# Routing map of a decoder step on one core: a job's tiles evicted one job later, a unit's weights split between its quarters

## The chip, the core and the metric

The kernel runs on one core of a Trainium2 chip. A core has a matrix engine (PE, with its weight loads listed apart as PEld), a vector engine (DVE), a scalar engine (ACT), a general engine (POOL) and a queue engine (SP). Each takes its instructions in order, and they meet at semaphores. The metric is the device time of one execution in microseconds (us).

## The reference

One decoder layer for 256 prompt tokens and 64 sample tokens. Attention and a gating unit come first; then a layer of 16,384 small experts, of which every token uses 16 for each of 8 heads; then a gated embedding. The part that matters here is the expert layer:

```python
s1, s2 = q1 @ k1.T, q2 @ k2.T                    # 128 keys each
v1, i1 = top_k(s1, 16);  v2, i2 = top_k(s2, 16)
sc, ci = top_k(all pairs v1 + v2, 16)
e = i1[ci // 16] * 128 + i2[ci % 16]             # expert of a pair of keys
g = softmax(sc)
out = sum over e of  g * gelu(u_tab[e] . x) * v_tab[e]
```

## The kernel before

For 240 prompt tokens the kernel does not gather experts. It goes through all of them densely: 128 "u" units give the activations of 128 experts each for all tokens, 128 "v" units multiply them back, and a routing map of tokens by experts, zero almost everywhere, weighs them in between. The map must stand in device memory before the first activations are weighed.

A unit is one 1 MB tile of weights (`w_raw`). `prepare(n, h)` fetches it at h = 0 by SP's queue and makes, for half h, a high part (`w_hi`, ACT, L683) and the rest (`w_lo`, DVE, L684), so that a product of three matmuls (`mm3`, L98 to L100) has full precision. A pool of four holds the halves' parts. `multiply(n, h, q)` does quarter q of half h: four chunks of three matmuls. A half is called a slot here, slot = 2n + h; the stage has 28 units, so slots 0 to 55. `finish(n)` takes a unit's sum through the activation function on ACT (L706).

The map is made in slots 42 to 55, in 30 jobs of 8 tokens. Job j has three steps:

- `one_hots(j)`: DVE compares the chosen keys with all keys (`e`, L762) and weighs the result (`p`, L763). Two buffers of each.
- `map_products(j)`: 16 short matmuls on PE (L775) into two tiles of PSUM, of the tag "s" for even and "o" for odd jobs; each tag has two buffers.
- the eviction, in the same function: two ACT instructions (L779) move the two tiles into half of `g_st`, a tile for 16 tokens with two buffers. After an odd job POOL writes `g_st` to device memory, `gd` (L786). The eviction into a buffer of `g_st` waits for the write of two tiles before.

The order is written out by hand: instructions of PE, DVE and ACT stand on each engine as the code issues them (`manual_schedule`, L931). In a slot with map jobs the loop goes over the two quarters: `multiply`, then (in a unit's first quarter) `finish` of the unit before, then for each job that is due `one_hots(job + 1)` and `map_products(job)` with its eviction. Behind both quarters stands `prepare` of the slot three ahead (L953). Jobs are due evenly: one in a quarter, and in two of the 28 quarters two.

Behind the stage four more units run without jobs; then the first tile of the map is read back (`fetch_g`, L839) and its activations weighed (`weights`, L842), and the long part with u and v units begins.

Of the kernel before, what the change touches and what calls it, by code (L numbers as in the profile page):

```python
# [52 lines left out]
def _build(ctx, tc, nc, a):  # L53
# [16 lines left out]
    def psum(tag, cols, parts=P):  # L70
        t = ps.tile([P, 512], F32, tag=tag, name="ps_" + tag)
        return t[:parts, :cols]
# [598 lines left out]
    def prepare(n, h):  # L671

        if h == 0:
            r = raw.tile([P, 16, P], F32, name="w_raw")
            o = order[n]
            src = a["uT"][o[1]] if o[0] == "u" else a["v_t"][o[1], o[2]]
            nc.sync.dma_start(r.rearrange("p a b -> p (a b)"), src)
            halves[n] = [r]
        r = halves[n][0]
        hi = hl.tile([P, 8, P], F32R, name="w_hi")  # L680
        lo = hl.tile([P, 8, P], F32R, name="w_lo")
        s = r[:, 8 * h : 8 * h + 8]
        act.activation(hi, s, AF.Copy)  # L683
        vec.tensor_sub(lo, s, hi.bitcast(F32))  # L684
        halves[n].append((hi, lo))
# [79 lines left out]

    def map_products(j):
        e, parts = oh.pop(j)
        tb, hb = divmod(j, 16 // NB)
        if hb == 0:
            oh["st"] = oh["pool"].tile([P, NK, 16], F32, name="g_st")  # L770
        for q in range(NB // 4):
            gp = psum("so"[j % 2], 512)
            for t in range(4):
                for k in range(2):
                    pe.matmul(  # L775
                        gp[:, t * P : t * P + P], e[:, 1, q, :, t], parts[:, k, q, :, t], start=k == 0, stop=k == 1
                    )
            b = hb * NB + 4 * q
            act.activation(  # L779
                oh["st"][:, :, b : b + 4].rearrange("p a t -> p t a"),  # L780
                gp.rearrange("p (t a) -> p t a", t=4),
                AF.Copy,
                scale=1.0 / WSC,
            )
        if hb == 16 // NB - 1:
            pool.dma_start(  # L786
                gd[:, :, tb * P : tb * P + P].rearrange("g p x -> p g x"),
                oh["st"].rearrange("p (g i) t -> p g (i t)", g=NG),
            )
# [125 lines left out]
    def front():  # L915

        for c in heads[6:]:
            yield from c
        yield from soften()
        picks = key_tables()  # L920
        yield 1.4
        shut(c_rt)
        state["xc"], state["xcp"] = open_pool("xc")
        xcp = state["xcp"]
        state["rows"] = [xcp.tile([P, D], F32, name=n) for n in ("xc", "xx")]
        state["xd"] = lambda: xcp.tile([P, P], F32, name="xd", bufs=2)
        open_tables(picks)
        yield 1.4
        one_hots(0)

    with tc.manual_schedule(engines={mybir.EngineType.DVE, mybir.EngineType.Activation, mybir.EngineType.PE}):  # L931
        for n in range(2):
            for h in range(2):
                prepare(n, h)


        steps, spent, job, first = front(), 0.0, 0, None
        for n in range(U1):
            for h in range(2):
                slot = 2 * n + h  # L940
                for q in range(2):
                    multiply(n, h, q)
                    if h == 0 and q == 0 and n:
                        finish(n - 1)
                    if first:
                        at_ = (2 * (slot - first) + q + 1) / (2 * (2 * U1 - first))
                        while job < JOBS and job < round(JOBS * at_):
                            if job + 1 < JOBS:
                                one_hots(job + 1)
                            map_products(job)  # L950
                            job += 1
                if first:
                    prepare((slot + 3) // 2, 1 - h)  # L953
                else:
                    while steps and spent < 1.4 * (slot + 1):
                        cost = next(steps, None)
                        if cost is None:
                            steps = None
                        else:
                            spent += cost  # L960
                    if steps:
                        prepare(n + 2, h)
                    else:
                        first = slot + 1
        prepare(U1 + 1, 1)
        n = U1
        shut(oh["close"])
        c_vp, vp = open_pool("vp")
        c_xc, (xc, xx) = state["xc"], state["rows"]
        tails = []  # L970
        for z in (A0, C):
            z = z[2][:, :, :, TP : TP + TD // 4].rearrange("p c h t -> p (c h) t")
            tails += [[z[:, 4 * k : 4 * k + 4] for k in (2 * i, 2 * i + 1)] for i in range(2)]
        sets = [
            Rows("c", c_e, c_g, xc, rcol[:, 2:3]),
            Rows("x", x_eg[:, 0].bitcast(I32), x_eg[:, 1], xx, rcol[:, 3:4]),
        ]
        steps = [(k, j, second) for second in (False, True) for k in sets for j in range(k.n)]
        rows = {}

        def row(m):
            if m < len(steps):
                k, j, second = steps[m]
                rows[m] = k.fetch(j, second)


        state["g"] = fetch_g(0, pool)
        to_c = rows_of(xc, state["xd"], slice(TP, T), 2)
        to_x = rows_of(xx, state["xd"], slice(0, XT), PH)
        load = weights(0, state["g"])  # L990
        for n in range(n, LEAD):
            finish(n - 1)
            for h in range(2):
                for q in range(2):
                    multiply(n, h, q)
                    next(to_c, None)
                if 2 * (n - U1) + h >= 4:
                    for _ in range(3):
                        next(load, None)
                if n == LEAD - 1 and h == 0:  # L1000
                    for m in range(3):
                        row(m)
                prepare(n + 2, h)
        for _ in to_c:
            pass


        END = len(order) - 10
        extra = lambda n: 0.65 * (order[n - 1][0] == "v")
        step_us = 2.4  # L1010
        total = sum(extra(n) for n in range(LEAD, END)) + 0.8 * GRP * NG + step_us * len(steps)
        m, spent, slots = 0, 0.0, 0
        sums_c = add_samples()
        sums_x = None
        last_norm = last_split()
        for n in range(LEAD, len(order)):
            finish(n - 1)
            if order[n][0] == "v" and order[n][2] == 0:
                for _ in load or ():
                    pass  # L1020
                load = None
            if order[n][0] == "u" and order[n - 1][0] == "v":
                coming, at_ = order[n - 1][1] + 1, 0
                groups[coming] = []
                load = weights(coming, state["g"])
            for h in range(2):
                multiply(n, h, 0)
                multiply(n, h, 1)
                if h == 0 and n > LEAD:
                    spent += extra(n)  # L1030
                next(to_x, None)
                if load and (at_ >= GRP or coming * GRP + at_ in acts):
                    if next(load, 0) is None:
                        at_ += 1
                        spent += 0.8 if at_ <= GRP else 0.0
                if m >= len(steps) - 16:
                    next(sums_c, None)
                if sums_x:
                    next(sums_x, None)
                if order[n][0] == "v" and order[n][1] == NG - 1 and order[n][2]:  # L1040
                    next(last_norm)
                slots += 1
                while m < len(steps) and (spent + step_us / 2 < total * slots / (2 * (END - LEAD)) or n >= END):
                    k, j, second = steps[m]
                    k.step(j, second, rows.pop(m))
                    row(m + 3)
                    m += 1
                    spent += step_us
                if m == len(steps) and not sums_x and n >= END:
                    sums_x = add_first()  # L1050
                if n + 2 < len(order):
                    prepare(n + 2, h)
        finish(n)
        for _ in last_norm:
            pass
# [154 lines left out]
```

## Time and profile before

| | us |
|---|---|
| median of 3 runs (lowest, highest) | 2134.97 (2132.25, 2137.13) |
| the profiled execution | 2136.97 |
| its span, first to last instruction | 2135.2 |
| the map's stage, slots 42 to 55 | 114.76 |
| PE busy over the span | 2101.2 (98%) |

The rows further down are from this one profiled execution. A line of the timeline gives the start, the duration, and in brackets the idle time of that engine before the instruction and what ended it. Matmuls overlap, so the time that one takes from PE is the distance from its start to the next start, not its duration. The granted clock is 1.00 at PE's upper level of 2.4 GHz and 0.50 at its lower one of 1.2 GHz.

### The profile page before, as it was taken

Reading aid. Unit: us, or ns where it says so; the run is one execution under the profiler, and the core shown is the slowest. Engines: PE = TensorE matmul, PEld = TensorE weight load, DVE = VectorE, ACT = ScalarE, POOL = GpSimd, SP = SyncE. Lnnn points to the kernel's source line nnn. Section 1 sums busy time; section 2 is a strip of 40 time slices with the busy share of each in tenths; the row PEclk is TensorE's granted clock in tenths of the full one; section 3 lists DMA queues with packets and bytes.
Section 4 is the critical chain, followed back from the end, with each engine's and each line's share of the span. In section 5 each row is a group of like instructions: output and inputs, shape, how many; then the busy total and the mean of one; then the engine's idle time right before and its main releaser. Section 6 shows DMA issues by size and latency. Waiting matters only on the chain. (4 is left out here: it accounts for less than half of the span.)

```text
span 2135.2 us, 41032 instructions
## 1 busy us (share of the span) xinstructions
PE 2101.2 (98%) x17106; PEld 2051.5 (96%) x17106; DVE 1714.6 (80%) x2563; ACT 1002.7 (47%) x1457; POOL 315.1 (15%) x231
## 2 busy tenths in 40 slices
PE   8999999999998899999999999999999999999999
PEld 7879999999998899999999999999999999999999
DVE  6574875699997768888888898898898888885754
ACT  5346554335446665444444444444444444434632
POOL 2000000000001111222222222122222222210000
PEclk9999999999999999999999999999999999999999
DMA  7312254333556688999989999999899898884452
GB/s 280 144 62 82 101 208 165 138 139 122 183 194 188 204 317 326 379 349 351 382 352 349 361 362 351 348 376 363 334 378 359 338 375 350 333 320 170 152 181 84
DMA packets 85209, 563.06 MB, mean 264 GB/s; under 512 B 9894, under 2 KB 14438, under 8 KB 22160
## 3 DMA queue, kind: packets, MB, share of 16 engines
q1 hardware_dynamic: 49936, 349.76, 44.1%
q0 software_dynamic: 29680, 191.81, 23.6%
q10 hardware_dynamic: 5408, 18.88, 2.3%
q8 instruction: 134, 2.20, 0.4%
q14 instruction: 51, 0.42, 0.1%
HBM read 541.58 MB, written 19.79 MB: 263 GB/s over the span
## 5 line engine op out<-in xcount | busy, mean ns | idle before, releaser
L683 ACT ACTIVATE w_hi<-w_raw 128x1024 fp32r<-128x1024 f32 x512 | 542.6, 1060 | 682.7 <-PE ps_o L99 362.8
L684 DVE TENSOR_TENSOR w_lo<-w_raw,w_hi 128x1024 fp32r<-128x1024 f32 x512 | 624.6, 1221 | 206.0 <-ACT w_hi L683 204.9
L98 PE MATMUL ps_mm<-a,w_hi 128*128 128x240 f32 (+1 forms) x1776 | 518.2, 292 | 2.1 <-ACT w_hi L191 1.7
L99 PE MATMUL ps_mm<-a,w_hi 128*128 128x240 f32 (+1 forms) x1776 | 518.7, 292 | 1.0 <-DVE a L123 1.0
L100 PE MATMUL ps_mm<-a,w_lo 128*128 128x240 f32 (+1 forms) x1776 | 516.6, 291 | 2.6 <-DVE w_lo L684 2.1
L98 PE MATMUL ps_mm<-c,w_hi 128*128 128x240 f32 (+1 forms) x1280 | 362.9, 283 | 0.0
L100 PE MATMUL ps_mm<-c,w_lo 128*128 128x240 f32 (+1 forms) x1280 | 361.2, 282 | 0.0
L99 PE MATMUL ps_mm<-c,w_hi 128*128 128x240 f32 (+1 forms) x1280 | 360.9, 282 | 0.0
L99 PEld LDWEIGHTS ps_mm<-a,w_hi 128*128 128x128 f32 x1776 | 336.7, 190 | 8.9 <-issue 6.6
L98 PEld LDWEIGHTS ps_mm<-a,w_hi 128*128 128x128 f32 x1776 | 336.8, 190 | 8.4 <-issue 4.8
L100 PEld LDWEIGHTS ps_mm<-a,w_lo 128*128 128x128 f32 x1776 | 336.8, 190 | 7.0 <-issue 3.2
L81 ACT ACTIVATE w_hi<-w_raw 128x1024 fp32r<-128x1024 f32 x150 | 158.6, 1059 | 282.2 <-PE ps_mm L99 188.8
L99 PE MATMUL ps_o<-wl,w_hi 128*128 128x240 f32 x1024 | 282.0, 275 | 1.1 <-DVE wl L849 1.1
L100 PE MATMUL ps_o<-wh,w_lo 128*128 128x240 f32 x1024 | 282.3, 276 | 0.0
L98 PE MATMUL ps_o<-wh,w_hi 128*128 128x240 f32 x1024 | 278.9, 272 | 0.0
L82 DVE TENSOR_TENSOR w_lo<-w_raw,w_hi 128x1024 fp32r<-128x1024 f32 x150 | 182.5, 1220 | 94.5 <-ACT w_hi L81 91.3
L100 PEld LDWEIGHTS ps_mm<-c,w_lo 128*128 128x128 f32 x1280 | 243.4, 190 | 0.2
L98 PEld LDWEIGHTS ps_mm<-c,w_hi 128*128 128x128 f32 x1280 | 243.5, 190 | 0.0
L99 PEld LDWEIGHTS ps_mm<-c,w_hi 128*128 128x128 f32 x1280 | 243.4, 190 | 0.0
L99 PEld LDWEIGHTS ps_o<-wl,w_hi 128*128 128x128 f32 x1024 | 192.7, 188 | 1.8 <-DVE wl L849 1.7
L98 PEld LDWEIGHTS ps_o<-wh,w_hi 128*128 128x128 f32 x1024 | 194.3, 190 | 0.0
L100 PEld LDWEIGHTS ps_o<-wh,w_lo 128*128 128x128 f32 x1024 | 194.3, 190 | 0.0
(382 smaller groups left out, 3792.5 us busy)
## 6 DMA issues: line engine op xcount, KB each, us to landing
w_raw<-in_uT SPq DMA_DIRECT2D x128, 1024.0 KB, 6.3
w_raw<-in_v_t SPq DMA_DIRECT2D x128, 1024.0 KB, 8.7
w_raw<-in_w_in SPq DMA_DIRECT2D x25, 1024.0 KB, 5.0
w_raw<-in_w_out SPq DMA_DIRECT2D x16, 1024.0 KB, 4.8
w_raw<-in_wq SPq DMA_DIRECT2D x16, 1024.0 KB, 4.8
w_raw<-in_w_gate SPq DMA_DIRECT2D x16, 1024.0 KB, 5.0
gd<-g_st POOLq DMA_DIRECT2D x15, 1024.0 KB, 6.5
g_t<-gd ACTq DMA_DIRECT2D x15, 960.0 KB, 8.0
```

The source lines that it names most:

```text
L81: last = act.activation(hi, s, AF.Copy)
L82: (lo_eng or vec).tensor_sub(lo, s, hi.bitcast(F32))
L98: pe.matmul(out, wh, xh, start=start, stop=False)
L99: pe.matmul(out, wh, xl, start=False, stop=False)
L100: pe.matmul(out, wl, xh, start=False, stop=stop)
L683: act.activation(hi, s, AF.Copy)
L684: vec.tensor_sub(lo, s, hi.bitcast(F32))
```

## The change

The eviction becomes a function of its own, `map_out(j, out)`, and the loop calls it one job later: behind `one_hots(job + 1)` and `map_products(job)` stands the eviction of job - 1. The last job is evicted behind the loop. `prepare` of the slot three ahead moves from behind the second quarter to behind the first, after that quarter's jobs.

```diff
     def map_products(j):
         e, parts = oh.pop(j)
-        tb, hb = divmod(j, 16 // NB)
-        if hb == 0:
-            oh["st"] = oh["pool"].tile([P, NK, 16], F32, name="g_st")
+        oh["out"] = []
         for q in range(NB // 4):
             gp = psum("so"[j % 2], 512)
+            oh["out"].append(gp)
             for t in range(4):
                 for k in range(2):
                     pe.matmul(
                         gp[:, t * P : t * P + P], e[:, 1, q, :, t], parts[:, k, q, :, t], start=k == 0, stop=k == 1
                     )
+
+    def map_out(j, out):
+        tb, hb = divmod(j, 16 // NB)
+        if hb == 0:
+            oh["st"] = oh["pool"].tile([P, NK, 16], F32, name="g_st")
+        for q, gp in enumerate(out):
             b = hb * NB + 4 * q
             act.activation(
                 oh["st"][:, :, b : b + 4].rearrange("p a t -> p t a"),
...
-        steps, spent, job, first = front(), 0.0, 0, None
+        steps, spent, job, first, out = front(), 0.0, 0, None, None
...
                             if job + 1 < JOBS:
                                 one_hots(job + 1)
                             map_products(job)
+                            if out:
+                                map_out(job - 1, out)
+                            out = oh["out"]
                             job += 1
-                if first:
-                    prepare((slot + 3) // 2, 1 - h)
-                else:
+                        if q == 0:
+                            prepare((slot + 3) // 2, 1 - h)
+                if not first:
                     while steps and spent < 1.4 * (slot + 1):
...
+        map_out(JOBS - 1, out)
         prepare(U1 + 1, 1)
```

Two engines get another order; PE, POOL and SP keep theirs. On ACT, at the first two slots of the stage, before (the two tiles of an even job are `ps_s`, of an odd job `ps_o`; jobs 0 to 5 follow each other):

```order
L779 ACTIVATE g_st_6977<-ps_s_6978 128x4x128
L779 ACTIVATE g_st_6977<-ps_s_6988 128x4x128
L779 ACTIVATE g_st_6977<-ps_o_7014 128x4x128
L779 ACTIVATE g_st_6977<-ps_o_7024 128x4x128
L683 ACTIVATE w_hi_7035<-w_raw_6924 128x1024
L779 ACTIVATE g_st_7055<-ps_s_7056 128x4x128
L779 ACTIVATE g_st_7055<-ps_s_7066 128x4x128
L779 ACTIVATE g_st_7055<-ps_o_7092 128x4x128
L779 ACTIVATE g_st_7055<-ps_o_7102 128x4x128
L683 ACTIVATE w_hi_7115<-w_raw_7113 128x1024
L706 ACTIVATE act_7132<-ps_mm_6958 128x240
```

and now:

```order
L683 ACTIVATE w_hi_6995<-w_raw_6924 128x1024
L784 ACTIVATE g_st_7033<-ps_s_6977 128x4x128
L784 ACTIVATE g_st_7033<-ps_s_6986 128x4x128
L784 ACTIVATE g_st_7033<-ps_o_7015 128x4x128
L784 ACTIVATE g_st_7033<-ps_o_7024 128x4x128
L683 ACTIVATE w_hi_7075<-w_raw_7073 128x1024
L784 ACTIVATE g_st_7113<-ps_s_7052 128x4x128
L784 ACTIVATE g_st_7113<-ps_s_7061 128x4x128
L706 ACTIVATE act_7129<-ps_mm_6958 128x240
L784 ACTIVATE g_st_7113<-ps_o_7095 128x4x128
L784 ACTIVATE g_st_7113<-ps_o_7104 128x4x128
L683 ACTIVATE w_hi_7156<-w_raw_7073 128x1024
```

A slot's `w_hi` stood behind the evictions of both of its jobs; now it stands behind that of the job before the slot's first, and the first slot's own stands ahead of any eviction.

On DVE, from the stage's first job (e_6954, job 0) on, before:

```order
L762 TENSOR_TENSOR e_6954<-i4_6912,sel0_6914 128x2048
L763 TENSOR_TENSOR p_6955<-e_6954,sel0_6914 128x2048
L762 TENSOR_TENSOR e_6973<-i4_6912,sel0_6914 128x2048
L763 TENSOR_TENSOR p_6974<-e_6973,sel0_6914 128x2048
L762 TENSOR_TENSOR e_7010<-i4_6912,sel0_6914 128x2048
L763 TENSOR_TENSOR p_7011<-e_7010,sel0_6914 128x2048
L684 TENSOR_TENSOR w_lo_7036<-w_raw_6924,w_hi_7035 128x1024
L762 TENSOR_TENSOR e_7051<-i4_6912,sel0_6914 128x2048
L763 TENSOR_TENSOR p_7052<-e_7051,sel0_6914 128x2048
L762 TENSOR_TENSOR e_7088<-i4_6912,sel0_6914 128x2048
L763 TENSOR_TENSOR p_7089<-e_7088,sel0_6914 128x2048
L684 TENSOR_TENSOR w_lo_7116<-w_raw_7113,w_hi_7115 128x1024
```

and now:

```order
L762 TENSOR_TENSOR e_6954<-i4_6912,sel0_6914 128x2048
L763 TENSOR_TENSOR p_6955<-e_6954,sel0_6914 128x2048
L762 TENSOR_TENSOR e_6973<-i4_6912,sel0_6914 128x2048
L763 TENSOR_TENSOR p_6974<-e_6973,sel0_6914 128x2048
L684 TENSOR_TENSOR w_lo_6996<-w_raw_6924,w_hi_6995 128x1024
L762 TENSOR_TENSOR e_7011<-i4_6912,sel0_6914 128x2048
L763 TENSOR_TENSOR p_7012<-e_7011,sel0_6914 128x2048
L762 TENSOR_TENSOR e_7048<-i4_6912,sel0_6914 128x2048
L763 TENSOR_TENSOR p_7049<-e_7048,sel0_6914 128x2048
L684 TENSOR_TENSOR w_lo_7076<-w_raw_7073,w_hi_7075 128x1024
L762 TENSOR_TENSOR e_7091<-i4_6912,sel0_6914 128x2048
L763 TENSOR_TENSOR p_7092<-e_7091,sel0_6914 128x2048
```

Each `w_lo` moved up by one `one_hots`: it stood behind the pairs made in both quarters of its slot and stands between them now.

## Rows read from the trace of the kernel before

**Rows 1.** Busy time by stretch: length, then for PE, PEld, DVE, ACT and POOL busy us and instructions, the granted clock, the DMA engines' busy share and GB/s. The first stretch is the map's stage, from its first matmul to that of slot 56.

```profile
640.95:755.71 114.76, 101.34 (x819) 97.20 (x817) 86.47 (x73) 72.03 (x79) 17.34 (x17) 0.94 0.63 190
760.00:800.00 40.00, 39.02 (x346) 38.48 (x345) 27.61 (x37) 27.08 (x52) 6.86 (x6) 1.00 0.94 356
800.00:1800.00 1000.00, 1000.00 (x8944) 1000.00 (x8943) 881.70 (x907) 452.75 (x574) 239.19 (x142) 1.00 0.92 358
```

**Rows 2.** Who waited for whom from 640 to 756 us: total us, times, longest.

```profile
DVE w_lo L684 <- ACT w_hi L683: 25.6, 14, 3.8
ACT g_st L779 <- PE ps_s L775: 21.0, 10, 2.7
ACT g_st L779 <- PE ps_o L775: 18.4, 12, 2.4
PEld L775 <- DVE p L763: 15.4, 13, 1.6
```

**Rows 3.** The timeline of PE in the stage: the start, then two slots with their products, the two bursts of a quarter with two jobs, and the last burst. An "x16" is the burst of one job.

```profile
640.95 0.27 PE L98 MATMUL ps_mm<-a,w_hi 128*128 128x240 f32 x1
643.13 2.03 PE L775 MATMUL ps_s<-p,e 128*128 128x128 f16 x16 [0.67 <-DVE p L763]
...
654.07 2.06 PE L775 MATMUL ps_o<-p,e 128*128 128x128 f16 x16 [1.07 <-DVE p L763]
655.88 0.36 PE L98 MATMUL ps_mm<-a,w_hi 128*128 128x240 f32 x1
657.31 2.06 PE L775 MATMUL ps_s<-p,e 128*128 128x128 f16 x16
659.13 0.36 PE L98 MATMUL ps_mm<-a,w_hi 128*128 128x240 f32 x1
660.44 0.27 PE L100 MATMUL ps_mm<-a,w_lo 128*128 128x240 f32 x1
661.80 2.07 PE L775 MATMUL ps_o<-p,e 128*128 128x128 f16 x16 [1.08 <-DVE p L763]
663.62 0.39 PE L98 MATMUL ps_mm<-c,w_hi 128*128 128x240 f32 x1
666.15 2.09 PE L775 MATMUL ps_s<-p,e 128*128 128x128 f16 x16
669.52 2.06 PE L775 MATMUL ps_o<-p,e 128*128 128x128 f16 x16 [1.28 <-DVE p L763]
...
753.90 2.06 PE L775 MATMUL ps_o<-p,e 128*128 128x128 f16 x16 [1.09 <-DVE p L763]
755.71 0.36 PE L98 MATMUL ps_mm<-a,w_hi 128*128 128x240 f32 x1
```

**Rows 4.** The timeline of ACT over the same slots.

```profile
655.22 2.02 ACT L779 ACTIVATE g_st<-ps_o 128x512 f32<-128x512 f32 x2 [2.44 <-PE ps_o L775]
657.02 1.07 ACT L683 ACTIVATE w_hi<-w_raw 128x1024 fp32r<-128x1024 f32 x1
657.98 0.37 ACT L706 ACTIVATE act<-ps_mm 128x240 f32<-128x240 f32 x1
658.52 2.02 ACT L779 ACTIVATE g_st<-ps_s 128x512 f32<-128x512 f32 x2 [0.17 <-ACT act L706]
```

**Rows 5.** The timeline of DVE over the same slots.

```profile
658.12 1.23 DVE L684 TENSOR_TENSOR w_lo<-w_raw,w_hi 128x1024 fp32r<-128x1024 f32 x1 [1.72 <-ACT w_hi L683]
659.27 1.22 DVE L762 TENSOR_TENSOR e<-i,sel 128x2048 f16<-128x2048 f16 x1
660.52 1.22 DVE L763 TENSOR_TENSOR p<-e,sel 128x2048 f16<-128x2048 f16 x1
661.66 1.22 DVE L762 TENSOR_TENSOR e<-i,sel 128x2048 f16<-128x2048 f16 x1
```

**Rows 6.** The granted clock in stretches of 2 us (length, PE busy and matmuls, clock, DMA share, GB/s), at the first and the last fall of the stage.

```profile
662.00:664.00 2.00, 2.00 (x18) 0.95 0.52 152
664.00:666.00 2.00, 2.00 (x12) 0.50 0.00 0
...
754.00:756.00 2.00, 2.00 (x18) 0.99 1.03 240
756.00:758.00 2.00, 2.00 (x12) 0.50 1.00 414
758.00:760.00 2.00, 2.00 (x14) 0.65 0.51 162
760.00:762.00 2.00, 2.00 (x20) 1.00 1.01 285
```

**Rows 7.** The map's writes: POOL's issues of `gd` (duration in ns least, median, most; first and last start), and the time from issue to landing of the accesses to `g_st`, least, median, most; then one issue in the timeline of POOL.

```profile
L786 POOL DMA_DIRECT2D gd<-g_st x15: 1152/1152/1212, 649.8 to 757.5; - x15
DMA to landing us min/median/max: 6.0/6.5/7.5
697.57 1.15 POOL L786 DMA_DIRECT2D gd<-g_st  x1 [6.74 <-ACT g_st L779]
```

**Rows 8.** DVE at that issue, and the read of the map's first tile behind the stage with DVE's first instruction that uses it.

```profile
697.12 1.22 DVE L762 TENSOR_TENSOR e<-i,sel 128x2048 f16<-128x2048 f16 x1
...
764.78 0.56 POOL L839 DMA_DIRECT2D g_t<-gd  x1 [6.16 <-PE ps_tr L798]
771.15 0.72 DVE L854 TENSOR_TENSOR act<-act,g_t 128x240 f32<-128x240 f32 x2
```

## The prediction

> **What bounds the kernel now.** I read the stages first [rows 1]. From 800 to 1800 us PE is busy all the time, so what comes earlier there shortens the kernel by as much. In the map's stage PE is busy 101.3 of 114.76 us, DVE 86.5 and ACT 72.0: no engine is full, and the clock is 0.94. Something goes round in a circle. The waits name its links [rows 2]: PE waits for `p` of DVE 13 times, DVE for `w_hi` of ACT 14 times, ACT for PE's products 22 times.
>
> One round can be followed through the three timelines. Products start at 654.07 [rows 3]; ACT can take the first tile at 655.22, 1.15 us later, is done with both when `w_hi` starts at 657.02 (1.80), and DVE's `w_lo` starts at 658.12 (1.10) [rows 4, 5]. Then `w_lo` takes 1.15 us to the next start, at 659.27, and `e` and `p` until the products of the next odd job start at 661.80, 2.53 us. The sum is 1.15 + 1.80 + 1.10 + 1.15 + 2.53 = 7.73 us, exactly the distance 654.07 to 661.80. So a slot takes 7.73 us because the split of the weights stands behind the slot's last eviction and ahead of the next `one_hots`.
>
> What PE itself needs is less. A burst of products takes 655.88 - 654.07 = 1.81 us, a quarter of a unit 657.31 - 655.88 = 1.43 us [rows 3]. A slot of two quarters and two jobs is 2 x (1.43 + 1.81) = 6.48 us.
>
> **The change, part by part.** No instruction is added or dropped, and each keeps its duration; what changes is which waits end last.
>
> *The circle.* With the new order `w_hi` waits for the eviction of job j - 1 only, and `w_lo` stands behind `p` of job j + 1 and ahead of `e` of job j + 2. From the start of products j - 1 the chain is the same 7.73 us, but it now ends at products j + 2, three jobs later, for which PE needs 3 x 3.24 = 9.72 us. It has 2.0 us to spare.
>
> *DVE.* In a slot it does `w_lo` (1.15) and two pairs of `e` and `p`, each 661.66 - 659.27 = 2.39 us [rows 5]: 5.93 us in 6.48. It may stand idle 0.55 us a slot before PE waits. A pair may start when the products two jobs back have freed its buffers, and must be done when its own products start: 1.43 + 1.81 + 1.43 = 4.67 us, in which 2.39 fit, and 2.39 + 1.15 = 3.54 fit too. I put this wait at nothing.
>
> *ACT.* Four evictions in two pairs of 1.80, `w_hi` 0.96 (657.02 to 657.98) and, in every second slot, `finish` of about 0.4 [rows 4]: 4.8 us in 6.48. The later eviction holds its two PSUM buffers longer, but the tag is used again only two jobs on: from the end of products j to products j + 2 there are 1.43 + 1.81 + 1.43 = 4.67 us, and the eviction needs 1.80 with at most 0.96 of `w_hi` and 0.4 of `finish` ahead of it. Nothing again.
>
> *The sum for the stage.* 28 quarters of 1.43 are 40.0 and 30 bursts of 1.81 are 54.3; the first wait stays, since nothing stands ahead of job 0's pair that could move (quarter over at 642.3, products at 643.13 [rows 3]): 0.8. That makes 95.1 us in place of 114.76, a gain of 19.7. The same from the other side: 114.76 - 94.3 = 20.5 us are lost now, of which 15.4 are the waits of the weight loads for `p` [rows 2], and the rest comes from the clock.
>
> *The clock.* It falls to 1.2 GHz after a burst that had waited: after that of 661.80, where the next quarter takes 666.15 - 663.62 = 2.53 us in place of 1.43 [rows 3, 6]. The last burst, at 753.90, had waited too, and the fall behind it lasts from 756 to 759.3 [rows 6], outside the stage; it costs half of 3.3 us, 1.7. Without the waits I expect these falls to go. The gain in the stage already holds those inside it; the last adds 1.7, so 21.4 in all. Against that I set one fall that stays, most likely in a quarter with two jobs, where 3.6 us of bursts stand together: 1.1 us. And 0.3 for a map write that comes late (below). Net gain 20.0 us.
>
> *Moved past the queues.* `prepare` brings SP's fetch of the weights forward by half a slot; the tile is not needed for some slots, and DMA is busy 63% of the stage [rows 1], so it neither gains nor costs. In 114.76 - 20 = 95 us the same bytes need a share of about 0.63 x 114.8 / 94.8 = 0.76. POOL's write of `gd` still follows the eviction of the odd job; at the end of the stage job 29 is evicted right behind its products, as before, so the read of the first map tile at 764.78 and its use at 771.15 [rows 8] move with the rest.
>
> *A wait that the trace of before doesn't show.* An eviction into `g_st` waits for the write of two tiles before. A write lands 6.0 to 7.5 us after its issue [rows 7]. The circle of two buffers covers two slots: eviction 1.80, `w_hi` 0.96, eviction 1.80, 0.4 to POOL's issue and the landing L, about 5.0 + L, against 12.96 us of PE. It binds from L = 8.0 on if everything lies well, a little earlier where a `finish` stands between. At 7.5, the most seen, it costs nothing; if the denser traffic makes it 9, it costs 7 pairs of slots x 1.0 = 7 us. I take the median, 6.5, and 0.3 for single late ones.
>
> A row bears on this: the issue of 697.57 ran while DVE was in an `e` (697.12 to 698.34), and took 1.15 us as all others did (1152 to 1212 ns) [rows 7, 8]. The Trainium skill, SBUF — State Buffer, section "SBUF: two separate sides", warns that a DMA issued by POOL gets no descriptors while DVE holds the port that they share, in certain forms of instruction. With DVE now busy over 90% of the stage it would speak against the change: each write would be late by up to a pair of `e` and `p`. By the rule L would be 6.5 + 2.4 = 8.9 and the gain smaller by some 6 us. By the row it is not, and the sum goes without it.
>
> **The profiled execution** took 2136.97 us, 2.0 above the median of 2134.97. Less 20.0 it is 2117.0; against the median, which the result will be compared with, 2115.0. That is the forecast.
>
> **Rivals.**
>
> *Slower: the map's writes become the bound.* Mechanism as above, in slots 46 to 55: ACT stands at the first eviction of a tile until the write of two tiles before has landed, and `w_hi`, `w_lo` and `p` queue behind it. The stage is then 7 x (5.0 + L) + 0.8. L = 9 gives 98.8, 10 gives 105.8, and from L = 11.3 it is slower than now; L = 12 gives 119.8 and 2140 us. For it: two slots now give the circle 15.5 us and then 13.0; weights and writes share the DMA. Against it: a range of 6.0 to 7.5 with the queues 63% busy. For L between 8 and 10 I give 0.13 (2118 to 2126), beyond 11.3 0.02.
>
> *The clock doesn't recover.* If bursts alone make it fall, each fall costs 1.1 us; four to eight give 2118 to 2123. Against it: bursts without a wait, such as that of 657.31, were followed by a quarter at full rate (659.13 to 660.44, 12 matmuls) [rows 3]. 0.10.
>
> *The order opens less than it says.* DVE has 0.55 us of room in a slot; if it waits 1.0 for `w_hi`, PE loses 0.45 in 14 slots, 6 us: 2121. If the circle stays in the quarters with two jobs, about 2 x 1.5 = 3 us. 0.06.
>
> *The gain is given back behind the stage.* The map's first tile must land before 771.15 less the gain. If the units behind the stage wait for all of it, no change. PE keeps pace from 760 to 800 (39.0 of 40 us [rows 1]). 0.03.
>
> **How the numbers follow.** The forecast has 0.66 with its own range of 2111 to 2118: the best is 21.4 from the lowest run of before, 2132.25 - 21.4 = 2110.9. The range for 8 in 10 takes in the milder part of the rivals: writes at L = 9 and two falls more cost 9.2, 2124; so 2111 to 2125. What a measurement of this kernel can tell from no change is about 0.2%, 4.3 us. Faster than that are the forecast and nearly all of the next three (0.66 + 0.13 + 0.10 + 0.06, less 0.01); the same 0.03, slower 0.03.
>
> **What the profile of the changed kernel would show.** Right: the stage is 95 to 97 us long; PE's wait for `p` falls from 13 to one or two; DVE's wait for `w_hi` from 25.6 us to under 8; the distance of two bursts of odd jobs is 6.5 us; the clock is 0.98 or more there; ACT waits for PE, not for the write. Wrong: ACT's evictions of even jobs wait for `gd` (L too long), the clock is still at 0.94, PE waits for `p` in every slot, or PE stands still around the first use of the map behind the stage.

## The result, and the profile after

The changed kernel takes 2122.16 us (median of 5 runs, 2117.72 to 2123.03) beside 2136.72 us for the kernel before (5 runs, 2132.25 to 2138.84): a ratio of 0.9928 with an interval of 0.9913 to 0.9943. It is faster by 14.6 us; 20.0 were forecast. The time lies inside the wide range, 7.2 us above the forecast, and above the narrow range of 2111 to 2118 that had 0.66. Of the 7.2 us, 1.8 are the kernel before, whose median was 2134.97 in three runs and is 2136.72 in these five.

The profiled execution after took 2122.16 us (span 2120.4, clock 0.996). I cut both spans at two points that both kernels have, the start of the first products and the first matmul behind the stage:

| stretch, us | before | after | change | forecast |
|---|---|---|---|---|
| start to the first products | 643.13 | 641.85 | -1.3 | 0 |
| first products to the end of the stage | 112.58 | 95.94 | -16.6 | -18.3 |
| end of the stage to the end of the span | 1379.5 | 1382.6 | +3.1 | -1.7 |
| span | 2135.2 | 2120.4 | -14.8 | -20.0 |

(The forecast's -18.3 are its 19.7 less the 1.1 of a fall of the clock and the 0.3 of late writes.) The stage lacks 1.7 us to the forecast, and the stretch behind it 4.8. The first stretch belongs to no step of the change: three more executions of one or the other kernel in the experiments below gave 641.29, 643.36 and 643.07.

The stage, as a stretch (columns as in [rows 1]; from its first matmul to the first behind it), and the four waits of [rows 2], with the largest of the new ones:

```profile
639.67:737.79 98.12, 96.17 (x818) 94.02 (x817) 87.45 (x74) 73.13 (x80) 17.35 (x17) 0.98 0.72 231
```

```profile
ACT g_st L784 <- PE ps_s L774: 8.1, 9, 1.8
ACT g_st L784 <- DMA gd<-g_st: 7.9, 4, 3.6
ACT g_st L784 <- PE ps_o L774: 7.3, 10, 1.2
DVE w_lo L684 <- ACT w_hi L683: 3.3, 3, 2.4
...
PEld L774 <- DVE p L763: 1.8, 2, 1.0
...
PE ps_o L774 <- ACT g_st L784: 0.8, 1, 0.8
```

PE is busy for all but 2 us of the stage. The circle is open: DVE's wait for `w_hi` went from 25.6 us to 3.3, the weight loads' wait for `p` from 15.4 us in 13 places to 1.8 in 2. The wait of ACT for the map's writes, which the trace before did not show, is there: 7.9 us in 4 places.

PE's timeline shows the slots that answer to [rows 3], then the two places where a burst waited, and the end:

```profile
651.57 2.05 PE L774 MATMUL ps_o<-p,e 128*128 128x128 f16 x16
...
654.80 2.06 PE L774 MATMUL ps_s<-p,e 128*128 128x128 f16 x16
...
658.04 2.06 PE L774 MATMUL ps_o<-p,e 128*128 128x128 f16 x16
...
661.29 2.08 PE L774 MATMUL ps_s<-p,e 128*128 128x128 f16 x16
663.19 2.08 PE L774 MATMUL ps_o<-p,e 128*128 128x128 f16 x16
...
690.12 2.07 PE L774 MATMUL ps_o<-p,e 128*128 128x128 f16 x16 [0.84 <-ACT g_st L784]
...
715.33 2.06 PE L774 MATMUL ps_o<-p,e 128*128 128x128 f16 x16 [0.44 <-DVE p L763]
...
719.74 2.10 PE L774 MATMUL ps_s<-p,e 128*128 128x128 f16 x16
...
737.79 0.36 PE L98 MATMUL ps_mm<-a,w_hi 128*128 128x240 f32 x1
```

From 651.57 to 658.04 is one slot: 6.47 us, against 7.73 before and the 6.48 forecast. The bursts stand 3.23 to 3.25 us apart, and the quarter with two jobs at 661.29 has no wait between them.

### The profile page after: what moved, and what is told of

Its sections match the earlier page's. It is cut to its first block, busy times and chain, and to the rows that moved or that the text cites. A ratio compares the mean times of both kernels' runs of the same rounds, so it can differ in the third digit from the quotient of the medians.

```text
span 2120.4 us, 41033 instructions
## 1 busy us (share of the span) xinstructions
PE 2096.5 (99%) x17106; PEld 2048.2 (97%) x17106; DVE 1713.6 (81%) x2563; ACT 1002.2 (47%) x1457; POOL 314.0 (15%) x231
```

## The experiments

All of them compute the whole result; each is compared with runs of the kernel before on the same chip. Stage and rest are the second and third stretch of the table above, in the profiled execution.

| run | ratio, interval | stage | rest | ACT for writes (times) | DVE for the map's read |
|---|---|---|---|---|---|
| before | 1 | 112.58 | 1379.5 | 0 | 0 |
| before again | one run | 112.67 | 1378.4 | 0 | 0 |
| after | 0.9928, 0.9913 to 0.9943 | 95.94 | 1382.6 | 7.9 (4) | 3.0 |
| after again | 0.9922, 0.9908 to 0.9935 | 93.84 | 1380.1 | 8.4 (5) | 2.9 |
| after, third | 0.9925, 0.9910 to 0.9939 | 97.18 | 1380.0 | 11.6 (5) | 2.9 |
| split moved alone | 1.0006, 0.9997 to 1.0014 | 112.43 | 1380.9 | 0 | 3.8 |
| later eviction alone | 0.9913, 0.9900 to 0.9925 | 93.09 | 1380.6 | 4.1 (4) | 3.5 |
| the same again | 0.9921, 0.9907 to 0.9936 | 94.23 | 1381.7 | 6.2 (3) | 3.0 |
| three map tiles | 0.9951, 0.9938 to 0.9964 | 93.08 | 1388.2 | 0 | 9.5 |
| one map tile | one run | - | - | 93.6 (14) | - |
| writes from SP's queue | 0.9918, 0.9906 to 0.9930 | 98.6 | 1377.5 | 12.9 (4) | 0 |
| first use of the map later | 0.9914, 0.9900 to 0.9929 | 94.81 | 1377.6 | 9.6 (5) | 0.4 |
| later eviction, later use | 0.9896, 0.9881 to 0.9911 | 94.10 | 1378.3 | 6.5 (4) | 0.8 |
| before, later use | 0.9992, 0.9983 to 1.0001 | 112.45 | 1378.2 | 0 | 0 |

In two rows ("the same again", "first use of the map later") the view of the waits has 2.2 us in 2 and 5.8 in 4, and puts one more wait in each down to PE. These are the two, in that order:

```profile
728.88 1.96 ACT L784 ACTIVATE g_st<-ps_s 128x512 f32<-128x512 f32 x2 [4.04 <-PE ps_o L774]
```

```profile
683.92 1.96 ACT L784 ACTIVATE g_st<-ps_s 128x512 f32<-128x512 f32 x2 [3.84 <-PE ps_o L774]
```

An eviction of `ps_s` needs no product in `ps_o`; it needs the write of two tiles before, which was issued at 719.28 in the first case and landed 9.5 us later, at 728.8. So the table counts both with the writes.

My theory: the circle is cut because ACT no longer evicts a job's tiles ahead of `w_hi` behind the same job's products; the size is set by single late writes in the stage and by the map's read behind it. The rivals: the moved split does it, and DVE's load on the port that it shares with POOL holds the writes up.

**The split of the weights between the quarters, alone** (the eviction stays right behind its own products):

```diff
-                            if out:
-                                map_out(job - 1, out)
-                            out = oh["out"]
+                            map_out(job, oh["out"])
```

> The split of the weights between the quarters, alone; a job is evicted right behind its products as before. Theory (the later eviction opens the circle): w_hi now stands behind the eviction of the slot's first job, and w_lo ahead of the pair for the first job of the next slot, so the chain products, eviction, w_hi, w_lo, e, p of 7.73 us closes over two jobs again, one slot. The stage stays at 112 to 115 us, a slot at 7.7, the time within 0.2% of before (2132 to 2138). Rival (the place of the weights' split opens it): a slot of 6.5 us, a stage of 98 us or less, 2120 to 2124 us.

2138.29 us beside 2137.98: no difference. The circle stands as it was; these are PE's bursts of the kernel with this part alone:

```profile
712.20 2.06 PE L774 MATMUL ps_o<-p,e 128*128 128x128 f16 x16 [1.07 <-DVE p L763]
...
715.44 2.06 PE L774 MATMUL ps_s<-p,e 128*128 128x128 f16 x16
...
719.93 2.07 PE L774 MATMUL ps_o<-p,e 128*128 128x128 f16 x16 [1.08 <-DVE p L763]
```

712.20 to 719.93 is 7.73 us, the slot of [rows 3], with the same 1.07 us of waiting. Moving `w_hi` ahead in the program does nothing while the eviction ahead of it still waits for the newest products.

**The later eviction, alone** (the split stays behind both quarters):

```diff
-                        if q == 0:
-                            prepare((slot + 3) // 2, 1 - h)
-                if not first:
+                if first:
+                    prepare((slot + 3) // 2, 1 - h)
+                else:
```

> The later eviction alone; the split of the weights stays behind both quarters. Theory (the later eviction opens the circle): w_hi stands behind the eviction of the slot's first job and w_lo behind the pairs of both quarters, so the chain of 7.73 us ends three jobs on, where PE needs 9.72 us; a slot takes 6.5 us, the stage 96 to 99, the time is that of the whole change, 2118 to 2124 us. Rival (the place of the weights' split opens it): a slot stays near 7.7 us, 2131 us or more.

2118.91 us, all of the gain; the stage from its first matmul, expected at 96 to 99 us, took 95.3. The bursts of this kernel follow at the pace of PE:

```profile
656.32 2.05 PE L774 MATMUL ps_s<-p,e 128*128 128x128 f16 x16
...
659.55 2.06 PE L774 MATMUL ps_o<-p,e 128*128 128x128 f16 x16
...
662.79 2.07 PE L774 MATMUL ps_s<-p,e 128*128 128x128 f16 x16
```

So the half of the change that opens the circle is the eviction. To see whether the other half costs anything, both kernels ran again side by side:

> The later eviction alone once more, on the same chip and beside the whole change (the run after it). Theory (the split of the weights between the quarters adds nothing and makes loads of weights meet writes of the map): 1 to 3 us faster than the whole change, ratio 0.990 to 0.992, no load of weights issued within 0.5 us ahead of a write, stage 93 to 93.5 us from the first product on. Rival (the two differ by chance alone): within 1 us of the whole change.

> The changed kernel a third time, beside the later eviction alone. Theory (the split of the weights between the quarters makes loads meet writes): ratio 0.992 to 0.993; the write of the fifth tile is issued some 0.3 us behind a load of weights and lands 9 to 10 us later, as in both profiles so far; stage 93.8 to 96 us. Rival: no difference to the later eviction alone beyond 1 us.

2120.60 and 2121.75 us: not told apart by time. Three of the expected figures were missed: the stage of the eviction alone was 94.23 us, that of the third run of after 97.18, and its late write landed after 11.2 us. In their profiles the later eviction alone lost 0.2 and 1.3 us of the stage, the whole change 3.0, 0.9 and 4.3; whether the moved split costs anything stays open.

**A third map tile.** The third of every three tiles is the row buffer `xx`, idle in the stage, so that no eviction has to wait for the write of two tiles before:

```diff
-            oh["st"] = oh["pool"].tile([P, NK, 16], F32, name="g_st")
+            if tb % 3 == 2:
+                oh["st"] = state["rows"][1].rearrange("p (k t) -> p k t", t=16)
+            else:
+                oh["st"] = oh["pool"].tile([P, NK, 16], F32, name="g_st")
```

> The whole change, with a third buffer for the tile of 16 tokens (it takes a row buffer that is idle in this stage), so that an eviction waits for the write of three tiles before and not of two. Theory (what the stage lost against the forecast is the late writes of the map): ACT's waits for the write fall from 7.9 us to 0, PE's wait for an eviction goes, the stage falls from 98.1 to 95 to 96.5 us, the time by 1.5 to 3 us against the whole change, 2119 to 2121 us. Rival (the writes only fill time that ACT has to spare, and the stage lost to the clock and to the quarters with two jobs): the stage stays at 97.5 to 98.5 us, the time at 2122.

The waits for writes are gone, and the stage has its ideal 93.1 us: 27 quarters of 1.43 and 30 bursts of 1.81 behind the first products are 92.9. Yet the time is 2126.47 us, worse than after. The last write of the map goes out of `xx` here, at 738.38, between two gathers of rows by POOL (737.35 and 739.91). The read waits for that write and is issued only at 750.15; why the write takes so long is not shown. DVE, then PE, behind the stage:

```profile
759.77 0.73 DVE L862 TENSOR_TENSOR act<-act,g_t 128x240 f32<-128x240 f32 x2 [9.55 <-DMA g_t<-gd]
```

```profile
762.23 0.47 PE L806 MATMUL ps_tr<-ident,xd 128*128 128x128 f32 x1 [8.43 <-ACT xd L809]
```

The stage gained and the next stretch lost, over a path of which PE's own wait names only the last link: DVE waits for the read, ACT for DVE, PE for ACT's `xd`. A read that is late by 9.5 us puts 1388.2 where the kernel before needs 1378.2 to 1379.5. This miss showed me where the change's own gain went.

**The first use of the map later.** The units behind the stage begin to weigh with the map's first tile half a unit later, and then take four steps at a time:

```diff
-                if 2 * (n - U1) + h >= 4:
-                    for _ in range(3):
+                if 2 * (n - U1) + h >= 5:
+                    for _ in range(4):
```

> The whole change, with the weighing of the first activations begun half a unit later, four steps at a time in place of three. Theory (the 3 us given back behind the stage are the wait of DVE for the read of the map's first tile, which holds up ACT's row copies and PE's transposes): DVE's wait for the read falls from 3.0 us to under 0.5, PE's wait for the row copies from 2.5 to under 1 us, the fall of the clock there goes, the stretch behind the stage is 1378 to 1380 us in place of 1382.6, the time 2118 to 2120. Rival (the weighing itself is late wherever it stands, since the first v unit needs it): PE waits for the weighed activations at the first v unit instead, and the time stays at 2122 or rises.

2118.81 us. Two waits from 738 to 800 us in this kernel:

```profile
PE ps_tr L803 <- ACT xd L806: 1.6, 2, 1.2
...
DVE act L859 <- DMA g_t<-gd: 0.4, 1, 0.4
```

PE's 1.6 us are more than the 1 expected. The rest is 1377.6 us, 5.0 less than after and 1.9 less than before. The intervals of 0.9914 and of after's 0.9928 overlap, so the time alone doesn't show this gain. The same edit was put to the later eviction alone and to the kernel before, and before and after ran once more without it on the same chip:

> The later eviction alone (split of the weights behind both quarters, as before the change), and the weighing begun half a unit later. Theory (the two gains lie in different places and add up): the stage at the pace of PE, 93 us from the first product to the first matmul behind the stage, and 1377 to 1379 us behind it; ratio to before 0.989 to 0.991, some 2115 to 2118 us, faster than the whole change by 3 to 6 us. Rival (both remove the same wait, or the run without it is luck): the ratio stays at 0.991 to 0.993.

> The kernel before, with only the weighing begun half a unit later. Theory A (the wait for the map's first read is there before the change too, and the profiled execution of before happened to be without it): DVE's wait for the read stays under 0.5 us in the profile and the time falls by 2 to 4 us, ratio 0.998 to 0.999. Theory B (the change brings the wait, since the shorter stage lets the weights' loads meet the read): no change, ratio 0.9995 to 1.0005.

> The kernel before once more, for a second profile of the stretch behind the stage. Theory A (the wait for the map's first read is there before the change too): DVE waits 2 to 4 us for the read, and the stretch behind the stage is 1380 to 1382 us. Theory B (the change brings it): no wait, 1379 to 1380 us with the fall of the clock behind the last burst.

> The changed kernel once more, for a second profile and on the chip of the other runs of this call. Theory (its stage loses by single late writes of the map, which differ from execution to execution): the stage again 94 to 97 us from the first product on, one or two waits of PE for an eviction or for p, the landing of the latest write over 7 us; ratio 0.991 to 0.994. Rival (the 10.2 us of the latest write was an accident): no wait of PE for an eviction, 93 us, ratio 0.990 to 0.992.

With the later eviction it gives 2115.77 us beside 2136.26, 0.9896 (0.9881 to 0.9911): the fastest of all, 4.4 us under the 2120.13 of after on that chip, whose lowest run is 2119.10. Its stage is 94.10 us, above the expected 93. Its stretch behind the stage runs at full clock:

```profile
735.77:2114.10 1378.33, 1367.19 (x11909) 1363.80 (x11906) 1132.59 (x1197) 627.46 (x822) 273.36 (x163) 1.00 0.84 322
```

In the kernel before, where the read isn't waited for, the same edit gives 0.9992 (0.9983 to 1.0001): no clear gain, between the two theories. The second profile of before has no wait for the read either, so the wait is not one that the first profile missed by chance; what the edit gives after is this wait. After, run again, has a stage of 93.84 us, a little under the 94 that the theory had, and again one write that is waited for 9.5 us behind its issue: the 10.2 was no accident.

**One map tile.** To test the formula of the forecast for the writes, with one buffer the circle must cover one slot:

```diff
-            oh["st"] = oh["pool"].tile([P, NK, 16], F32, name="g_st")
+            oh["st"] = oh["pool"].tile([P, NK, 16], F32, name="g_st", bufs=1)
```

> The changed kernel with one buffer in place of two for the tile of 16 tokens, so that every tile's first eviction waits for the write of the tile before. It prices the wait that the prediction had as its slower rival. By that formula (two evictions 3.6 us, w_hi 1.0 where it stands between them, 0.4 to the issue, landing L of 6.1 to 7.0) a tile takes 10.1 to 12.0 us, 15 tiles some 150 to 175 us, the whole time 2175 to 2200 us, and ACT waits for the write 14 times. If instead the write is held up by the other transfers and not by its own latency, L falls below 6 us with the traffic spread over a longer stage, and the stage stays under 145 us.

2190.43 us. ACT's waits from 640 to 830 us, and the landing of the accesses to `g_st`:

```profile
ACT g_st L784 <- DMA gd<-g_st: 93.6, 14, 8.1
```

```profile
DMA to landing us min/median/max: 6.0/6.0/6.9
```

The 15 issues run from 650.48 to 809.09, so a round takes 158.61 / 14 = 11.3 us, and 5.0 + 6.0 is 11.0. The formula holds to 0.3 us, and with the circle closed every time the landing stays at 6.0 to 6.9.

**The map's writes issued by SP:**

```diff
-            pool.dma_start(
+            nc.sync.dma_start(
```

> The changed kernel with the writes of the map issued by SP's queue in place of POOL's. Theory A (the landing of a write is held up at POOL, which the Trainium skill, SBUF — State Buffer, section SBUF: two separate sides, says of DMAs issued there while DVE holds the shared port): the landing falls from 6.1 to 7 us to 5 or less, ACT no longer waits for a write, the stage is 93 to 93.5 us from the first product on, the first read of the map comes 1.5 us earlier, and the time falls by 2 to 3 us, ratio 0.990 to 0.991. Theory B (the landing is that of 16,384 pieces of 512 bytes on shared DMA engines): it stays at 6 us or more and the ratio at 0.991 to 0.993; the weights' loads that stand behind a waiting write in SP's queue come later, which the stage covers.

(A slip in that text: 1024 KB in pieces of 512 bytes are 2,048 of them, not 16,384.) 2118.76 us, a ratio of 0.9918 as Theory B has it. The waits for writes did not go, they grew:

```profile
ACT g_st L784 <- DMA gd<-g_st: 12.9, 4, 4.7
```

The stage is 98.6 us, longer than after. So POOL's hand in the issue isn't what makes writes late. Something else goes with it: the four writes that are waited for, issued at 673.15, 687.62, 702.63 and 716.37, are just the four that stand 0.4 to 0.7 us behind a load of weights in SP's queue, and the evictions start 9.7, 10.3, 8.9 and 8.5 us behind them. No eviction waited for any of the others. Behind the stage the read was not waited for, and the rest is 1377.5.

## Why the prediction was right, and where it fell short

**The circle: right.** 7.73 us became 6.47, PE's own 6.48. What opened it was the later eviction; the text had the new place of the split share in it, but the split alone opens nothing, and the eviction alone has the pace of the whole change.

**DVE, ACT and PSUM at nothing: right.** DVE is busy 87.45 of 98.12 us and the run with three tiles, where no eviction waits for a write, has the stage at 93.08, 0.2 above the sum of bursts and quarters. What the other runs lost in the stage, then, isn't DVE's or ACT's load.

**Late writes: the term was mis-sized.** I set 0.3 us for single ones beside the median landing; they cost 1.7 us in the profile after, and the fall of the clock behind the second burst that they held up 1.2 more. The two places where a burst waited both begin at such a write. ACT at the first, and POOL's issue of the write that it waits for:

```profile
683.59 1.96 ACT L784 ACTIVATE g_st<-ps_s 128x512 f32<-128x512 f32 x2 [3.61 <-DMA gd<-g_st]
...
708.75 2.02 ACT L784 ACTIVATE g_st<-ps_s 128x512 f32<-128x512 f32 x2 [1.85 <-DMA gd<-g_st]
```

```profile
673.25 1.15 POOL L791 DMA_DIRECT2D gd<-g_st  x1 [4.53 <-ACT g_st L784]
```

```profile
672.97 0.33 SPq L677 DMA_DIRECT2D w_raw<-in_uT  x1
```

SP's load of a `w_raw`, also 1024 KB, goes out at 672.97, 0.28 us ahead of the write at 673.25. That write is the slowest of the stage, and the landings of the accesses to `g_st` [rows 7] read now:

```profile
L791 POOL DMA_DIRECT2D gd<-g_st x15: 1152/1152/1215, 648.6 to 739.5; - x15
...
DMA to landing us min/median/max: 6.0/6.6/10.2
```

The median is where it was, 6.6; the most went from 7.5 to 10.2. The eviction at 708.75 waited for the write of 700.84, until 7.9 us behind its issue, and here too a load stands ahead, 1.05 us, at 699.79. The eviction at 683.59 is 3.61 us late, the burst at 690.12 starts 1.0 us later than its turn at 689.12, where its quarter was over. From the eviction at 708.75 the way goes over `w_hi` and `w_lo`, `e` and `p` to the burst at 715.33: 0.7 us, and behind that burst the clock falls:

```profile
716.00:720.00 4.00, 4.00 (x27) 3.89 (x25) 3.93 (x5) 2.91 (x4) 1.09 (x1) 0.66 0.96 369
720.00:724.00 4.00, 4.00 (x37) 3.94 (x36) 3.29 (x4) 2.37 (x3) 0.06 (x1) 0.92 0.83 236
```

The quarter there takes 719.74 - 717.14 = 2.60 us in place of 1.43, 1.17 more. 1.0 + 0.7 + 1.17 = 2.9 of the 3.0 us by which this stage exceeds 92.9. In the other two executions of after the same pair stands at 674.45 and 674.71, 674.20 and 674.36; the evictions that wait for it start 9.5 and 11.3 us behind the write, and the stage loses 0.9 and 4.3. Where the eviction alone is moved, that write is issued at 674.68 and the load follows only at 676.93: no eviction waits for it, and the loss is 0.2. There the pair comes close once, at 719.05 and 719.67, and the eviction behind it starts 7.3 us after the write; in the second run of the same kernel, at 718.63 and 719.28, it starts 9.6 us after, and with the later use added, at 717.33 and 717.97, 9.5 us after. In the whole change with the later use the pair stands at 673.08 and 673.38, and the eviction starts 10.5 us after. In the profile of the kernel before no load went out less than 1.6 us ahead of a write, and no write took more than 7.5 us. So a write issued within 0.7 us behind a load kept an eviction waiting until 9.5 us or more behind its issue in six of these seven executions, and until 8.5 us or more four times in the run with the writes from SP; none of them moved a load by itself. The text had said that the load, brought forward by half a slot, "neither gains nor costs"; by these profiles a load costs when it comes to stand right ahead of a write; but each of the two orders has one such place in its stage, and the times don't part them. The rival of the writes was thus there, not as every write slower (the median L stayed below 8) but as one or two a stage that meet a load of weights.

**The clock: right in the stage.** One fall was set at 1.1 and one came, 1.17, behind a waited burst. It did not come where I put it: the first quarter with two jobs, at 661.29, had no wait and no fall behind it. And a wait was not always followed by a fall: five other profiles (after again, the eviction alone twice, and the later use with either of them) show none in the stage, though single weight loads waited up to 1.3 us there.

**Behind the stage: this step failed.** The text said that the read of the map's first tile "and its use at 771.15 move with the rest", and counted 1.7 us for the last fall of the clock. The use moved forward, the read moved back. After the last burst the way to the use leads over a write, its landing, a read and its landing, here on POOL and then DVE:

```profile
739.54 1.15 POOL L791 DMA_DIRECT2D gd<-g_st  x1 [5.30 <-ACT g_st L784]
747.47 0.57 POOL L844 DMA_DIRECT2D g_t<-gd  x1 [6.78 <-DMA gd<-g_st]
```

```profile
754.82 0.73 DVE L859 TENSOR_TENSOR act<-act,g_t 128x240 f32<-128x240 f32 x2 [3.04 <-DMA g_t<-gd]
```

From the last burst's end at 737.79 to the use are 17.0 us. Before, the same use came 771.15 - 755.71 = 15.4 us behind the burst, without a wait; the read had been issued at 764.78, 9.1 us behind it [rows 8]. Now it is issued 747.47 - 737.79 = 9.7 us behind it. The time from its issue to its landing, before and after:

```profile
L839 POOL DMA_DIRECT2D g_t<-gd x1: 563/563/563, 764.8 to 764.8; - x1
...
DMA to landing us min/median/max: 4.8/4.8/4.8
```

```profile
L844 POOL DMA_DIRECT2D g_t<-gd x1: 566/566/566, 747.5 to 747.5; - x1
...
DMA to landing us min/median/max: 7.3/7.3/7.3
```

So the map's tile was there 13.9 us behind the burst, 1.5 ahead of its use, and is there 17.0 us behind it now. DVE comes to it at 754.82 - 3.04 = 751.78, 14.0 us behind the burst, 1.4 earlier than before, since PE and what follows it are no longer held back by the fall at 756 to 759.3 [rows 6]. 3.1 of a later landing and 1.4 of an earlier DVE, less the 1.5 to spare, are the wait of 3.0.

With the fall went also the place of SP's loads of weights. Two loads before, the first ahead of the read at 764.78 and the second behind it, then the one ahead of the read after:

```profile
760.34 0.33 SPq L677 DMA_DIRECT2D w_raw<-in_v_t  x1
...
765.45 0.33 SPq L677 DMA_DIRECT2D w_raw<-in_v_t  x1
```

```profile
745.99 0.33 SPq L677 DMA_DIRECT2D w_raw<-in_v_t  x1
```

In the three executions of before (one with the later use) the clock falls behind the last burst, two loads go out 4.6 and 9.7 us behind its end, and the read goes out 0.6 to 0.7 us ahead of the second: no wait. In the other profiles (one map tile apart) they go out 3.5 and 8.2 us behind it. In the six of these that have two map tiles, the use at its old place and the writes on POOL's queue, the read comes 1.1 to 1.7 us behind the second load, and DVE waits 2.9 to 3.8 us. With the writes issued by SP the read goes out 0.5 us ahead of that load, 7.7 us behind the burst, and is not waited for. The split alone is one of the six: its last burst had not waited, and no fall came behind it. So it is the missing fall, and not the shorter stage, that goes with the wait. What I counted as a gain of 1.7 us turned into a wait, and the wait is passed on: ACT and then PE wait for `xd`, and in this execution the clock falls behind that wait:

```profile
757.27 0.33 PE L803 MATMUL ps_tr<-ident,xd 128*128 128x128 f32 x1 [1.93 <-ACT xd L806]
```

```profile
756.00:760.00 4.00, 2.73 (x17) 2.73 (x18) 3.46 (x9) 2.72 (x7) 0.00 (x0) 0.78 1.00 424
760.00:764.00 4.00, 4.00 (x31) 4.00 (x31) 2.92 (x7) 3.08 (x8) 0.00 (x0) 0.80 0.99 358
```

The experiments bear this out from both sides. With the use half a unit later, or the read not waited for at all (writes from SP), the rest is 1377.5 to 1378.3 us. With the wait of 2.9 to 3.8 it is 1380.0 to 1382.6, the split alone with its unchanged stage among them. With 9.5 it is 1388.2. I had the rival "the gain is given back behind the stage", at 0.03, but as a matter of all or nothing; what came was a part of it, some 2 to 5 us over the 1377.5 to 1378.3 in each execution of after.

**The signs.** Of the signs of being right, the circle's pace, the waits for `p` and `w_hi` and the clock of 0.98 showed; the stage was 98.12 us and not 95 to 97. Two signs of being wrong showed as well: evictions of even jobs waited for `gd` four times, and PE stood still around the first use of the map.

**The sum, then.** Over the three executions of after the stage takes 95.65 us on average and the rest 1380.9; over before, before again, and before with the later use, 112.57 and 1378.7. 16.9 less 2.2 is 14.7 us, and 14.6 was measured. Of the 5.3 us that 14.7 lacks to 20.0, the stage lacks 18.3 - 16.9 = 1.4, and the stretch behind it 1.7 + 2.2 = 3.9.

**DVE's port: misread.** I took the rule of the Trainium skill (SBUF — State Buffer, section "SBUF: two separate sides") to cover DVE's instructions here, and priced it at L = 8.9. The same section says that `tensor_tensor` has no 2-port mode, and that it was not seen to stall a DMA where `tensor_copy` was. DVE's `e`, `p` and `w_lo` are all of that form (TENSOR_TENSOR in [rows 5]), so the rule gave no reason to expect a loss. The trace agrees: with DVE busy 89% of the stage the 15 issues still take 1152 to 1215 ns and the median landing is 6.6 us; issued by SP, the writes are waited for longer, not less.

**Open.** That a load of weights just ahead is what makes a write of the map, or the read of its first tile, late goes by the order in the traces; no run moved a load alone. Whether the moved split costs a microsecond, the times don't tell.

## What to carry to other kernels

Where no engine is full, follow one round through the engines and add up its links. If the sum is the distance of two rounds, look for the link that waits for the newest result; here that was the eviction, and moving what stood behind it changed nothing. Ahead of a gain, look for what at its end goes out to memory and back, and reckon when it will land and when its user will come; a stall that is to go may have been its cover. Moving the first use by half a unit took 2 to 5 us off the stretch behind the stage here. A wait that is sized by a median is sized wrongly where one late transfer among fifteen stops a chain: ask which other transfer can be issued just ahead of it.

## What was not expected of the hardware

A write of 1024 KB that mostly lands in 6.0 to 7 us took 10.2 us when a load of 1024 KB had been issued 0.28 us ahead of it, and up to 11.2 us in the other executions of the same order, while the mean DMA share of the stage was only 0.72; issued 2.2 us ahead of that load it kept nobody waiting. And a wait of PE of 1.7 to 2.7 us behind the stage was followed by a fall of the granted clock in some executions (0.79 from 756 to 764 us in after and in the first run of the later eviction alone) and in others by none (1.00 in the other two of after), with the same order of instructions in the three of after.
